# An encoder layer on one core: the sample's pointwise convolution as block-sum products, with the prompt's jobs in another order

## The chip, the cores and the metric

One Trainium2 chip, one core. The metric is device time in microseconds (us) of one launch, the median of the runs shown. The whole layer is one program, and each engine (TensorE or PE, VectorE or DVE, ScalarE or ACT, GpSimd or POOL, SyncE or SP) has a list of instructions of its own.

## The reference

Two sequences, a sample of 1024 tokens and a prompt of 512, go through the same layer with model width 2048:

```python
h = rms_norm(x, norm_g)
z = h @ w_in                                   # 2048 x 5632
c_val, c_glu, c_gate, q, k, v, a_gate = split(z)
# conformer group, 1024 channels
u = c_val * sigmoid(c_glu)
u = depthwise_conv(u, 31 taps) + b_dw
conv_out = (silu(layer_norm(u, ln_g, ln_b)) @ w_pw) * silu(c_gate)    # w_pw 1024 x 1024
# attention group, 8 heads of 128, 2 kv heads, window of 128 keys to each side, a sink per head
attn_out = banded_sink_attention(rope(q), rope(k), v, sink) * silu(a_gate)
y = rms_norm(x + concat(conv_out, attn_out) @ w_out, final_norm_g)    # w_out 2048 x 2048
```

The products are wanted at fp32 accuracy.

## The kernel before, in words

**Three passes for one product.** An fp32 operand is split into a high and a low part: `Encoder.parts` (L446-453) has ACT write the high part with a copy (L449) and DVE the low part with a subtraction (L450). A product is then hi by hi, hi by lo and lo by hi, three matmuls of 128x512 into one PSUM bank. A chunk of weights is loaded into a `raw` tile, and its two parts go into an `hl` tile of 128x1024 each (three such tiles, `NHL`). Tokens sit split in 28 `t` tiles.

**Seven products of block sums.** For the sample's in-projection and out-projection, class `Unit` (L91-250) takes two blocks of output columns, two halves of the inner dimension and two halves of the tokens, and uses the seven products P1 to P7 of sums of blocks in place of eight. The weight side is made in `make0` to `make3`: `make1` subtracts 128x512 blocks (L138), splits the first half of the new operand and then the second. The token sums S1 to S4 and plain blocks A11, A12, A22 are stored, loaded and split (`block_sums`, `load_sum`, `token_sum`). Each product has 12 matmuls (L191), and `tap` and `add` gather the results (L217, L237). Where the order is `ALONE`, it is P1, P2, P6, P5, P7, P3, P4.

**Plain jobs.** A `Job` (L320ff, matmuls at L587) is one block of 128 output columns with 512 tokens: 48 matmuls for the prompt's in-projection, 24 for the pointwise convolution, whose inner dimension is 1024. The sample's pointwise convolution (class `Post`, `first_jobs`) is 16 jobs of 24 matmuls, in two halves of 512 tokens: `prepare` does the layer norm, `normed` stores the result in `cs_d`, `fetch` loads it again and splits it, `pointwise` (L1395) multiplies the product with the gate, and `mixed` stores it.

**Work beside the matmuls.** The depthwise convolution, the attention, the norms and the block sums are generators in three lanes (`attn`, `conv`, `prep`, class `Lane`). After each group of three matmuls `tick` gives every lane credit at its rate, and a lane with credit emits its next step. `drain` or `until` emits all that is left of a lane, or enough of it, at once. One channel block of the depthwise convolution is 31 taps: two on ACT (L912, L913) and 29 on DVE (L917), 128x512 each for the prompt, and a sum (L919). A block of attention is scores (`s`, L1044), mask and maximum on DVE (L1047), exponentials on ACT (L1058), transposes (`pt`, L1078), a split of the transposed block (`a<-pt`) and the products with the values (`pv`, L1073).

**What sets the order.** The code is emitted in one pass, and a scheduler puts each engine's instructions in a fixed list by dependencies and priority. Making weights (`w_prep`, L546) has a priority that moves it up by 400 places of the emitted order (`URGENT`); the high part of a weight chunk is made as soon as an `hl` tile is free. `store_later` and `turn_over` put small steps behind marks. DMAs are issued by SP, each waiting for one that is eight earlier.

**The stages around the change.** The prompt's in-projection (`prompt.jobs`, L1118ff) begins with 12 attention jobs (keys, values, queries) and goes on for eight rounds of GLU, value, conv gate and attention gate. Job 18 (`PM`) calls `prepare`: the sample's convolution is finished, the two layer norms and the first `fetch` go to the prep lane, the sample's gating of the attention (`attention_sums`, L1178) and the prompt's attention groups to the attn lane; the conv lane's rate is 0.5 from there. The prompt's taps enter the conv lane as their value jobs finish. Then come the 16 pointwise jobs, and the eight units of the out-projection on the attention half (`over[0]`) and eight on the convolution half (`over[1]`).

Of the kernel before, what the change touches and what calls it, by code (L numbers as in the profile page):

```python
# [13 lines left out]
P = 128  # L14
# [3 lines left out]
NC = C // P  # L18
# [72 lines left out]
class Unit:  # L91
# [148 lines left out]
    def finish(self, n):  # L240
        e = self.e
        part, d = self.part[n[0]][n[1]], self.d.pop(n)
        if self.total:

            e.add_into(d, part)
            e.later.append([self.landing, self.done(n[0], n[1], d)])
        else:
            e.store_later(part, d)
# [415 lines left out]
class Sequence:  # L664
# [196 lines left out]
    def val(self, i, accs):  # L861
        e, nc = self.e, self.e.nc
        nc.vector.tensor_tensor(self.sig, accs[0], self.sig, ALU.mult)
        e.store_later(self.h_d[i], self.sig, lambda: e.conv.add(self.taps(i)))
# [254 lines left out]
    def jobs(self):  # L1119
# [5 lines left out]
            job(GATE + i, lambda acc: self.silu_out(self.gate_d[i], acc)),  # L1125
# [6 lines left out]
        gate = lambda h: [job(AG + h, lambda acc: self.silu_out(self.ag_d[h], acc))]  # L1132
        attn = kv(0) + kv(1) + sum((query(h) for h in range(HEADS)), [])
        attn[0].before.append(self.rope_tables)
        convs, gates = [conv(i) for i in range(NC)], [gate(h) for h in range(HEADS)]
        return attn + sum((c + g for c, g in zip(convs, gates)), [])


class Mix:
# [55 lines left out]

    def fill(self):

        e = self.e
        e.T = {}
        held = deque()  # L1200

        def load(step):
            if step < 7:
                held.append(self.load_sum(SUMS[ALONE[step]], 1, True, e.F))

        def put(step):
            for j, x in enumerate(held.popleft()):
                self.token_sum(SUMS[ALONE[step]], 1, j, x)

        load(0)  # L1210
        load(1)
        for step in range(4):
            yield 2 * LOAD
            put(step)
            load(step + 2)
        self.put, self.load = put, load
# [82 lines left out]

class Post:  # L1300
# [4 lines left out]
    def __init__(self, e, seq, t0, out):  # L1305
        self.e, self.seq, self.t0, self.out = e, seq, t0, out
        self.cs, self.mix, self.made = {}, {}, {}
        self.cs_d = [e.tc.dram_tile([P, 2, self.N], F32, name=f"cs{seq.s}_{t0}_{i}") for i in range(NC // 2)]
# [52 lines left out]
    def normed(self, i, t):  # L1361
        self.e.store(self.cs_d[i], t)
        self.kept = i + 1

    kept = 0

    def fetch(self):

        e = self.e
        held = deque()  # L1370

        def load(i):
            if i < NC // 2:
                held.append(e.F([2, self.N]))
                e.nc.sync.dma_start(held[-1], self.cs_d[i])

        load(0)
        load(1)
        for i in range(NC // 2):
            yield LOAD  # L1380
            t = held.popleft()
            load(i + 2)
            for j in (0, 1):
                self.cs[2 * i + j] = self.parts(t[:, j])
                yield 1500
# [11 lines left out]

    def mixed(self, i, f):
        self.e.store(self.out.xT[i][:, self.t0 : self.t0 + self.N], f)
# [206 lines left out]
def encoder(ctx, tc, a):  # L1606
# [3 lines left out]
    halves = [Post(e, sample, 0, mix), Post(e, sample, TP, mix)]  # L1610
# [83 lines left out]
    def change(before, unit, nxt):  # L1694

        held = {}
        rooms = (e.F, e.F, e.F, None, e.F, e.F, None)

        def load(step):
            held[step] = mix.load_sum(SUMS[ALONE[step]], 0, False, rooms[step])  # L1700

        def follow(step):
            for j, x in enumerate(held.pop(step)):
                mix.token_sum(SUMS[ALONE[step]], 0, j, x)
            if step < 3:
                load(step + 4)

        def begin():
            e.attn.drain()
            load(2)  # L1710
            load(3)

        before.before.append(e.prep.drain)
        before.after[3] = [lambda: load(0)]
        before.after[5] = [lambda: load(1)]
# [80 lines left out]
    def prepare():  # L1796
# [3 lines left out]
        e.prep.add(halves[0].fetch())  # L1800
# [5 lines left out]
    pace(pj[PM], RATES[4])  # L1806
    jobs = sum(items, []) + [[j] for j in pj]
# [3 lines left out]
    for n, half in enumerate(halves):  # L1811
        fj = half.first_jobs()
# [101 lines left out]
```

## Time and profile before

| | |
|---|---|
| median of 3 runs | 2115.74 us (2115.11 to 2118.36) |
| profiled execution | 2115.94 us, span 2114.2 us, mean granted clock 0.997 |
| PE busy | 2080.8 us, 9330 matmuls |
| DVE busy | 1683.7 us, 2581 instructions |
| ACT busy | 1098.4 us, 1794 instructions |
| last prompt job ends, pointwise begins | 1450.2 us |
| pointwise ends, out-projection begins | 1549.7 us |

The profile is of one execution. Rows of groups give line, engine, operation, tile names and shapes, a count, busy time and mean duration, and then the idle time before them with what ended it. Rows of the timeline give start and duration in us, with the idle time before in brackets. A run of back-to-back instructions is one row with a count, and the start of the next row tells what the run really took, since the durations of successive instructions overlap by some tens of ns. Rows of windows give the busy time of PE, PE's weight loads, DVE, ACT and POOL, then the granted clock, the DMA engines' share and GB/s.

### The profile page before, as it was taken

How to read it: one execution, taken by the hardware profiler on the slowest of the kernel's cores; microseconds unless marked ns; L12 is line 12 of the kernel's file. 1: busy time of each engine (PE TensorE's matmuls, PEld its weight loads, DVE VectorE, ACT ScalarE, POOL GpSimd, SP SyncE). 2: the span in 40 equal slices, each digit the busy share in tenths (PEclk: the TensorE clock that was granted, in tenths of full speed). 3: DMA queues.
4: the chain of work that ended last, by engine and by line, in shares of the span. 5: the costliest groups of instructions: out<-in, count | busy, mean ns of one | idle time of the engine just before them, and what ended most of it. 6: DMA issues, size and time to landing. Idle time of an engine off the chain costs nothing.

```text
span 2114.2 us, 26783 instructions
## 1 busy us (share of the span) xinstructions
PE 2080.8 (98%) x9330; PEld 1708.0 (81%) x9330; DVE 1683.7 (80%) x2581; ACT 1098.4 (52%) x1794; POOL 104.8 (5%) x124
## 2 busy tenths in 40 slices
PE   8999999999999999899999999999999999999998
PEld 7878888888888888688888888777888888887886
DVE  8658799988899898889887775667899677986553
ACT  7475445333555655655556775335454565563232
POOL 0001110000011111000000000000000001110000
PEclk9999999999999999999999999999999999999999
DMA  8888878754667777854465546886877469798962
GB/s 289 305 295 242 229 181 278 263 191 155 216 184 182 185 163 212 268 171 156 151 215 162 192 159 208 315 313 205 265 257 240 135 206 267 189 279 290 314 196 80
DMA packets 236408, 465.17 MB, mean 220 GB/s; under 512 B 22128, under 2 KB 79856, under 8 KB 236272
## 3 DMA queue, kind: packets, MB, share of 16 engines
q1 hardware_dynamic: 218992, 431.99, 61.4%
q0 software_dynamic: 17280, 31.46, 9.3%
q8 instruction: 73, 1.20, 0.2%
q14 instruction: 63, 0.52, 0.1%
HBM read 319.19 MB, written 144.18 MB: 219 GB/s over the span
## 4 chain that ended last, share of the span: by engine, by line
PE 76%; DMA 8%; DVE 7%; issue 5%; ACT 2%; POOL 1%; SPq 1%; ACTq 0%; POOLq 0%; DVEq 0%
PE a L191 22%; PE c L191 11%; PE a L587 10%; PE b L191 6%; PE c L587 5%; PE b L587 5%; DMA a<-ag_d 3%; PE s L1044 2%; PE pv L1073 2%; PE a L1564 2%; PE s L1564 2%; PE s L191 2%; DVE hl L450 2%; DVE f L917 1%; PE pt L1078 1%
## 5 line engine op out<-in xcount | busy, mean ns | idle before, releaser
L191 PE MATMUL a<-t,hl 128*128 128x512 f32 x2640 | 633.3, 390 | 4.6 <-ACT u L217 3.2
L191 PEld LDWEIGHTS a<-t,hl 128*128 128x128 f32 x2640 | 493.8, 188 | 110.8 <-ACT u L217 5.7
L450 DVE TENSOR_TENSOR hl<-raw,hl 128x1024 fp32r<-128x1024 f32 (+1 forms) x330 | 337.7, 1023 | 178.8 <-ACT hl L449 177.9
L449 ACT ACTIVATE hl<-raw 128x1024 fp32r<-128x1024 f32 (+1 forms) x330 | 296.3, 898 | 332.0 <-DVE raw L138 58.0
L917 DVE SCALAR_TENSOR_TENSOR f<-f,c_w_dw,f 128x1024 f32<-128x1024 f32 (+1 forms) x464 | 454.5, 1010 | 1.1 <-ACT f L912 0.8
L587 PE MATMUL a<-t,hl 128*128 128x512 f32 x1344 | 329.2, 394 | 1.2 <-DVE hl L450 0.9
L191 PE MATMUL c<-t,hl 128*128 128x512 f32 x1320 | 318.7, 389 | 0.7 <-ACT g L217 0.7
L587 PEld LDWEIGHTS a<-t,hl 128*128 128x128 f32 x1344 | 248.4, 188 | 53.0 <-DVE hl L450 2.3
L191 PEld LDWEIGHTS c<-t,hl 128*128 128x128 f32 x1320 | 247.7, 188 | 52.8 <-ACT g L217 1.3
L587 PE MATMUL c<-t,hl 128*128 128x512 f32 x672 | 167.3, 396 | 0.7 <-DVE hl L450 0.5
L587 PE MATMUL b<-t,hl 128*128 128x512 f32 x672 | 164.4, 393 | 1.3 <-DVE hl L450 1.3
L191 PE MATMUL b<-t,hl 128*128 128x512 f32 x660 | 161.3, 390 | 0.0
L587 PEld LDWEIGHTS b<-t,hl 128*128 128x128 f32 x672 | 124.4, 188 | 27.0 <-DVE hl L450 2.1
L587 PEld LDWEIGHTS c<-t,hl 128*128 128x128 f32 x672 | 124.7, 189 | 25.8 <-DVE hl L450 1.0
L191 PEld LDWEIGHTS b<-t,hl 128*128 128x128 f32 x660 | 123.4, 188 | 25.2
L217 ACT ACTIVATE u<-a 128x512 f32<-128x512 f32 x114 | 67.4, 592 | 78.8 <-PE a L191 64.4
L217 ACT ACTIVATE g<-a 128x512 f32<-128x512 f32 x106 | 62.8, 592 | 74.9 <-PE a L191 68.2
L1564 PE MATMUL a<-hl,t 128*128 128x512 f32 x192 | 75.0, 390 | 1.6 <-DVE g L1395 1.6
L1058 ACT ACTIVATE p<-p,tiny 128x384 f32<-128x384 f32 (+1 forms) x96 | 54.5, 570 | 33.0 <-DVE tiny L1055 21.8
L346 ACT ACTIVATE hl<-raw 128x1024 fp32r<-128x1024 f32 x44 | 46.3, 1052 | 35.8 <-DMA raw<-w_in 12.8
L449 ACT ACTIVATE a<-pt 128x512 fp32r<-128x512 f32 x64 | 37.9, 592 | 50.4 <-PE pt L1078 50.1
L1047 DVE CUSTOM_DVE_ANT_0 p<-s,c_mask,c_attn_sink 128x384 f32<-128x384 f32 (+1 forms) x96 | 51.0, 568 | 14.9 <-PE s L1044 14.7
(319 smaller groups left out, 2534.9 us busy)
## 6 DMA issues: line engine op xcount, KB each, us to landing
raw<-w_in SPq DMA_DIRECT2D x171, 512.0 KB, 4.8
raw<-w_out SPq DMA_DIRECT2D x64, 256.0 KB, 4.1
raw<-w_out SPq DMA_DIRECT2D x31, 512.0 KB, 5.5
a<-xT_s SPq DMA_DIRECT2D x50, 256.0 KB, 4.7
raw<-w_pw SPq DMA_DIRECT2D x24, 512.0 KB, 4.9
f<-x_s SPq DMA_DIRECT2D x16, 512.0 KB, 6.9
f<-y_d SPq DMA_DIRECT2D x16, 512.0 KB, 5.8
y_s<-f SPq DMA_DIRECT2D x16, 512.0 KB, 4.7
```

The source lines that it names most:

```text
L191: nc.tensor.matmul(acc, hl[:, l, o, j, :], toks[j][:, r], start=name in FRESH and j == 0 and q == 0, stop=name in LAST and j == HALF - 1 a ...
L217: nc.scalar.activation(t, bank, AF.Copy)
L346: e.nc.scalar.activation(t[:, 0], raw, AF.Copy)
L449: nc.scalar.activation(hi, x, AF.Copy)
L450: nc.vector.tensor_tensor(lo, x, hi.bitcast(F32), ALU.subtract)
L587: nc.tensor.matmul(job.acc[0], hl[:, l, kk // HALF, kk % HALF, :], r, start=i == 0 and p == 0, stop=i == nk - 1 and p == 2,)
L917: nc.vector.scalar_tensor_tensor(t, h[:, j : j + T], w(j), t, ALU.mult, ALU.add)
L1044: nc.tensor.matmul(ps[:, 0:n], qs[:, x, h], k[y][:, keys], start=p == 0, stop=p == 2)
L1047: nc.vector.tensor_tensor_reduce(p[:, 0:n], ps[:, 0:n], mask, SCALE, e.sink[:, g * GROUP + h : g * GROUP + h + 1], ALU.add, ALU.max, accum ...
L1058: nc.scalar.activation(p[:, 0:n], p[:, 0:n], AF.Exp, bias=nm[:, h : h + 1], accum_out=l[:, h : h + 1])
L1073: nc.tensor.matmul(pv, v[x][:, vs], pt[:, y], start=i == 0 and p == 0, stop=i == last and p == 2)
L1564: nc.tensor.matmul(acc, self.mix[self.KS[i]][:, m, b * P : (b + 1) * P], part[l].rearrange("p a b -> p (a b)"), start=i == 0 and p == 0, s ...
```

## The change: block sums for the pointwise convolution, and rests for two lanes

- The 16 jobs of the pointwise convolution become four units of seven products, 12 matmuls each: 336 matmuls in place of 384. A new class `Norm` stores the normed tokens (`pair_d`), makes and stores their sums S1 to S4 on the prep lane (`sums`), loads and splits the first three token operands (`fill`), and multiplies the results with the gate (`gated`). The operands of the steps 3 to 6 are put during the last prompt job.
- The prompt's jobs: the 12 attention jobs stay first; then all eight pairs of GLU and value, then all eight pairs of conv gate and attention gate.
- Ahead of the first unit, `rest` emits at once what the attn lane has left until the sample's attention is gated and two blocks of the prompt's attention are finished, and what the conv lane has left until seven of the prompt's eight channel blocks are convolved. During the four units both lanes have rate 0. The eighth channel block's taps enter at `over[0][2]`.
- The conv lane's rate is 1.0 from the twelfth job from the end; `conv_sums` moves to `over[0][1]`; `change`, which refills the token tiles from one unit to the next, now also serves the way from the last pointwise unit to `over[0][0]`.

```diff
         return [
             job(GLU + i, self.glu),
             job(VAL + i, lambda acc: self.val(i, acc)),
-            job(GATE + i, lambda acc: self.silu_out(self.gate_d[i], acc)),
         ]
...
-        convs, gates = [conv(i) for i in range(NC)], [gate(h) for h in range(HEADS)]
-        return attn + sum((c + g for c, g in zip(convs, gates)), [])
+        return attn + sum((conv(i) for i in range(NC)), []) + sum((gate(h) for h in range(HEADS)), [])
...
+class Norm:
+    def sums(self):
+        e, nc = self.e, self.e.nc
+        for j in range(HALF):
+            x = [e.F([TS]) for _ in range(2)]
+            for t, k in zip(x, (j, j + HALF)):
+                nc.sync.dma_start(t, self.xT[k])
+            yield 2 * LOAD
+            self.block_sums(0, j, *x)
+            yield 4000
...
+    def units(self):
+        e = self.e
+        def one(o):
+            done = lambda t, c, z: self.gated(o + c, t, z)
+            return Unit(e, e.a["w_pw"], (o, o + 1), 0, None, done)
+        return [one(o) for o in range(0, NC, 2)]
+
+    def gated(self, o, t, z):
...
+        nc.sync.dma_start(g, self.seq.gate_d[o][:, cols])
+        def steps():
+            nc.vector.tensor_tensor(z, z, g, ALU.mult)
+            yield
+            e.store(self.mix.xT[o][:, cols], z)
...
-        e.prep.add(halves[0].fetch())
+        e.prep.add(norm.sums())
+        e.prep.add(norm.fill())
...
+    pace(pj[-12], RATES[3])
+    def ahead():
+        e.prep.drain()
+        norm.load(3)
+        norm.load(4)
...
+    pj[-2].before.append(ahead)
+    for step in range(3, 7):
+        pj[-1].ticks[HALF * (step - 2) - 1] = lambda step=step: refill(step)
...
+    pw = norm.units()
+    def rest():
+        until(lambda: mix.gated == HALF and prompt.finished >= 2, e.attn)
+        until(lambda: prompt.convolved >= NC - 1, e.conv)
+
+    pw[0].before.append(rest)
+    pace(pw[0], 0.0)
+    pace(pw[0], 0.0, e.attn)
+    jobs += [[u] for u in pw]
...
+    over[0][2].before.append(lambda: e.conv.add(prompt.taps(NC - 1)))
+    over[0][1].before.append(lambda: e.prep.add(mix.conv_sums()))
+    change(pw[-1], pw[-1], over[0][0], 1, (e.F, e.F, None, e.F, e.F, None, e.F))
```

The line numbers of the changed kernel are a few higher than before: L449 and L450 are L450 and L451 there, L917 is L921, L1044 is L1048, L1047 is L1051, L1078 is L1082, L1159 to L1162 are L1164 to L1167, L1178 is L1183.

Three places of the program, as the scheduler leaves them.

First, DVE among the prompt's gate jobs. Before, around the end of the prompt's jobs, its list goes from taps (`f` with `c_w_dw`) and small steps of a softmax to the low parts of two weight chunks (`hl_12230`, `hl_12282`):

```order
L917 SCALAR_TENSOR_TENSOR f_11774<-f_11694,c_w_dw,f_11774 128x512 x6
L1062 TENSOR_TENSOR tiny_11864<-tiny_11864,tiny_11863 128x4
L917 SCALAR_TENSOR_TENSOR f_11774<-f_11694,c_w_dw,f_11774 128x512
L1063 RECIPROCAL tiny_11865<-tiny_11864 128x4
L917 SCALAR_TENSOR_TENSOR f_11774<-f_11694,c_w_dw,f_11774 128x512 x5
L450 TENSOR_TENSOR hl_12230<-raw_12134,hl_12230 128x1024
L450 TENSOR_TENSOR a_12075<-pt_12070,a_12075 128x512
L450 TENSOR_TENSOR hl_12282<-raw_12183,hl_12282 128x1024
```

Now, between the low parts `hl_11896` and `hl_11997`, the first chunks of two successive prompt jobs, DVE has 19 taps, two gate products of the sample's attention (L1183) and twelve instructions of block sums (L1164 to L1167). The end of that stretch:

```order
L921 SCALAR_TENSOR_TENSOR f_11539<-f_11505,c_w_dw,f_11539 128x512 x7
L1164 TENSOR_TENSOR u_11684<-f_11590,f_11591 128x512
L921 SCALAR_TENSOR_TENSOR f_11539<-f_11505,c_w_dw,f_11539 128x512
L1165 TENSOR_TENSOR g_11685<-u_11684,f_11590 128x512
L1167 TENSOR_TENSOR g_11687<-f_11590 128x512
L1166 TENSOR_TENSOR u_11686<-f_11591,g_11685 128x512
L921 SCALAR_TENSOR_TENSOR f_11539<-f_11505,c_w_dw,f_11539 128x512 x2
L451 TENSOR_TENSOR hl_11997<-raw_11899,hl_11997 128x1024
```

What moved: the block sums of the normed tokens and of the attention, with the gate products ahead of them, now stand between two successive weight chunks, where before there were taps and softmax steps.

Second, DVE at the beginning of the pointwise convolution. Before, in its first jobs, each job's weights (`hl_`) follow the last ones after a few other instructions:

```order
L450 TENSOR_TENSOR hl_12376<-raw_12285,hl_12376 128x1024
L1395 TENSOR_TENSOR g_12329<-a_12331,g_12329 128x512
L450 TENSOR_TENSOR hl_12430<-raw_12338,hl_12430 128x1024
L917 SCALAR_TENSOR_TENSOR f_12305<-f_12220,c_w_dw,f_12305 128x512 x2
L450 TENSOR_TENSOR t_1740_12316<-f_12287,t_1740_12316 128x512
L450 TENSOR_TENSOR a_12404<-pt_12399,a_12404 128x512
L450 TENSOR_TENSOR t_1745_12346<-f_12287,t_1745_12346 128x512
L917 SCALAR_TENSOR_TENSOR f_12305<-f_12220,c_w_dw,f_12305 128x512
L1395 TENSOR_TENSOR g_12370<-c_12372,g_12370 128x512
L450 TENSOR_TENSOR hl_12492<-raw_12379,hl_12492 128x1024
```

Now, in the first unit, the operand `hl_12565` is made in two halves (`make1`); its first half and `hl_12573` stand soon after `hl_12442`, and its second half stands at the end of this piece, behind the last taps, token operands (`t_`) and the last three transposed blocks of attention (`a<-pt`):

```order
L451 TENSOR_TENSOR t_1782_12478<-f_12388,t_1782_12478 128x512
L451 TENSOR_TENSOR a_12524<-pt_12519,a_12524 128x512
L451 TENSOR_TENSOR t_1783_12500<-f_12432,t_1783_12500 128x512
L451 TENSOR_TENSOR t_1784_12503<-f_12432,t_1784_12503 128x512
L451 TENSOR_TENSOR t_1785_12506<-f_12433,t_1785_12506 128x512
L451 TENSOR_TENSOR t_1786_12509<-f_12433,t_1786_12509 128x512
L451 TENSOR_TENSOR a_12535<-pt_12530,a_12535 128x512
L138 TENSOR_TENSOR p_12561<-raw_12360,raw_12307 128x512
L138 TENSOR_TENSOR raw_12307<-raw_12307,p_12561 128x512
L451 TENSOR_TENSOR a_12546<-pt_12541,a_12546 128x512
L451 TENSOR_TENSOR hl_12565<-p_12561,hl_12565 128x512
L451 TENSOR_TENSOR hl_12609<-raw_12307,hl_12609 128x512
```

From `hl_12442` (not counted) to the second half of `hl_12565` DVE now has, counted in its list: 58 taps; 37 other instructions of 128x512 (4 subtractions of weight blocks, 20 token operands, 11 low parts of weights, keys, queries and transposed blocks, 2 sums of a channel block); one low part of 128x1024 (`hl_12573`); 8 instructions of mask and maximum; and some 20 of a few elements. The taps of two channel blocks that lay spread between the weights of many jobs now stand in one stretch of the first unit.

Third, PE at the same place. Before, the first pointwise jobs (L587, reading `hl_12230` and the following) have a product of scores between them:

```order
L587 MATMUL b_12278<-t_1585_11242,hl_12230 128x512 x3
L587 MATMUL b_12278<-t_1587_11256,hl_12230 128x512 x3
L587 MATMUL b_12278<-t_1602_11326,hl_12230 128x512 x3
L1044 MATMUL s_12236<-f_11735,a_12153 128x384 x3
L1044 MATMUL s_12242<-f_11735,a_12153 128x384 x3
L587 MATMUL b_12278<-t_1604_11342,hl_12230 128x512 x3
```

Now P1 (`a_12555` from `hl_12442`), P2 and P5 (the first half of `hl_12565`) have been issued with the attention of the two prompt blocks among them, and then P6 needs the second half of `hl_12565`:

```order
L1082 MATMUL pt_12541<-c_ident,p_12401 128x128
L1082 MATMUL pt_12541<-c_ident,p_12407 128x128
L1082 MATMUL pt_12541<-c_ident,p_12450 128x128
L1082 MATMUL pt_12541<-c_ident,p_12456 128x128
L1077 MATMUL pv_12518<-a_12546,f_11840 128x512 x3
L191 MATMUL a_12555<-t_1706_12004,hl_12565 128x512 x3
L191 MATMUL a_12555<-t_1707_12007,hl_12565 128x512 x3
L191 MATMUL a_12555<-t_1708_12010,hl_12565 128x512 x3
L191 MATMUL a_12555<-t_1709_12013,hl_12565 128x512 x3
```

On PE, 36 matmuls of the first unit and the attention of two prompt blocks stand between the last prompt job and P6: 12 score products of 256 and 12 of 384, 20 transposes and 15 products with the values.

More of the change, by code (lines that the diff above doesn't have):

```diff
@@ L241, in finish @@
         e = self.e
-        part, d = self.part[n[0]][n[1]], self.d.pop(n)
+        d = self.d.pop(n)
+        part = self.part and self.part[n[0]][n[1]]
         if self.total:
-            e.add_into(d, part)
+            if part is not None:
+                e.add_into(d, part)
             e.later.append([self.landing, self.done(n[0], n[1], d)])
@@ L863, in val @@
         nc.vector.tensor_tensor(self.sig, accs[0], self.sig, ALU.mult)
-        e.store_later(self.h_d[i], self.sig, lambda: e.conv.add(self.taps(i)))
+        if i < NC - 1:
+            e.store_later(self.h_d[i], self.sig, lambda: e.conv.add(self.taps(i)))
+        else:
+            e.store_later(self.h_d[i], self.sig)
     def gated(self, i):
@@ L1361, in normed @@
     def normed(self, i, t):
[L1362 to L1385, printed above, removed]
+        self.e.store(self.out.pair_d[i][:, :, self.t0 : self.t0 + self.N], t)
     def parts(self, f):
@@ L1692, in switch, with change @@
             u.after.setdefault(at, []).append(lambda step=step: follow(step))
-    def change(before, unit, nxt):
+    def change(before, unit, nxt, g, rooms):
         held = {}
-        rooms = (e.F, e.F, e.F, None, e.F, e.F, None)
+        ahead = 4 if before is not unit else 3
         def load(step):
-            held[step] = mix.load_sum(SUMS[ALONE[step]], 0, False, rooms[step])
+            held[step] = mix.load_sum(SUMS[ALONE[step]], g, False, rooms[step])
         def follow(step):
             for j, x in enumerate(held.pop(step)):
-                mix.token_sum(SUMS[ALONE[step]], 0, j, x)
-            if step < 3:
-                load(step + 4)
+                mix.token_sum(SUMS[ALONE[step]], g, j, x)
+            if step + ahead < 7:
+                load(step + ahead)
         def begin():
-            e.attn.drain()
-            load(2)
-            load(3)
+            if before is not unit:
+                e.attn.drain()
+            else:
+                load(0)
+                load(1)
+            for step in range(2, ahead):
+                load(step)
         before.before.append(e.prep.drain)
-        before.after[3] = [lambda: load(0)]
-        before.after[5] = [lambda: load(1)]
+        if before is not unit:
+            before.after.setdefault(3, []).append(lambda: load(0))
+            before.after.setdefault(5, []).append(lambda: load(1))
         unit.before.append(begin)
```

85 lines of the change are left out of this document (43 added, 42 removed).

## The prediction

> **What bounds the kernel now.** I read the profile's page first: the busy times, the slices of the span and the chain that ended last.
>
> ```profile
> PE 2080.8 (98%) x9330; PEld 1708.0 (81%) x9330; DVE 1683.7 (80%) x2581; ACT 1098.4 (52%) x1794; POOL 104.8 (5%) x124
> PE   8999999999999999899999999999999999999998
> DVE  8658799988899898889887775667899677986553
> PE 76%; DMA 8%; DVE 7%; issue 5%; ACT 2%; POOL 1%; SPq 1%; ACTq 0%; POOLq 0%; DVEq 0%
> ```
>
> TensorE is busy for 98% of the span, so a matmul saved is worth its time only if PE finds the next one ready. VectorE has 20% of room over the whole, but its slices go from 5 to 9 tenths, so I asked for the stretch that the change touches: the last prompt jobs (to 1450 us) and the pointwise convolution (1450 to 1550). The columns are length, busy PE, PEld, DVE, ACT and POOL, clock, DMA share and GB/s.
>
> ```profile
> 1340.00:1360.00 20.00, 20.00 (x89) 16.55 (x89) 16.45 (x26) 4.65 (x6) 0.00 (x0) 1.00 0.99 343
> 1360.00:1380.00 20.00, 19.27 (x84) 15.31 (x83) 5.35 (x6) 6.08 (x8) 0.00 (x0) 1.00 0.82 292
> 1480.00:1500.00 20.00, 19.98 (x91) 16.59 (x90) 19.35 (x36) 6.00 (x13) 0.00 (x0) 1.00 0.80 254
> 1560.00:1580.00 20.00, 19.82 (x89) 15.75 (x88) 19.93 (x32) 7.91 (x12) 0.00 (x0) 1.00 0.84 279
> ```
>
> In the pointwise stage and behind it DVE is full (19.35 and 19.93 of 20 us) and PE loses next to nothing. That works only because, in DVE's list, the weights' low parts never have more in front of them than PE can cover. What PE waits for in the last prompt jobs (1300 to 1445) is small:
>
> ```profile
> PE s L1044 <- ACT a L449: 2.6, 1, 2.6
> PE b L587 <- DVE hl L450: 0.6, 1, 0.6
> PE c L587 <- DVE hl L450: 0.5, 1, 0.5
> PE a L587 <- DVE hl L450: 0.5, 1, 0.5
> PE a L587 <- ACT hl L449: 0.2, 1, 0.2
> ```
>
> Does DVE run its list in the order in which it stands? The timeline of DVE around 1443 has a low part of weights, a transposed block and the next low part, as the piece of the list from before has them:
>
> ```profile
> 1413.47 4.73 DVE L917 SCALAR_TENSOR_TENSOR f<-f,c_w_dw,f 128x512 f32<-128x512 f32 x7
> 1418.11 1.22 DVE L450 TENSOR_TENSOR hl<-raw,hl 128x1024 fp32r<-128x1024 f32 x1
> ...
> 1443.79 1.21 DVE L450 TENSOR_TENSOR hl<-raw,hl 128x1024 fp32r<-128x1024 f32 x1
> 1444.93 0.68 DVE L450 TENSOR_TENSOR a<-pt,a 128x512 fp32r<-128x512 f32 x1
> 1445.53 1.21 DVE L450 TENSOR_TENSOR hl<-raw,hl 128x1024 fp32r<-128x1024 f32 x1
> ```
>
> It does, and these rows give the real cost of an instruction from start to start: 4.64 us for 7 taps, 0.66 each; 1.14 for a 128x1024 low part (1443.79 to 1444.93); 0.60 for a 128x512 one (1444.93 to 1445.53). [...]
>
> **The change, part by part.** *Matmuls removed.* The timeline of PE gives the pace:
>
> ```profile
> 1306.37 11.04 PE L587 MATMUL b<-t,hl 128*128 128x512 f32 x48
> 1317.25 11.04 PE L587 MATMUL a<-t,hl 128*128 128x512 f32 x48
> ```
>
> 48 matmuls take 10.88 us from start to start, 0.2267 each. Of 384 go 48: -10.9 us. The list of PE is otherwise of the same length. The evacuations, the gate products and the splitting of the normed tokens that are exchanged for others are work of DVE and ACT beside the matmuls: at 0.60 and 1.14 us I count about 37 us of DVE work gone (16 low parts of 1024, the 16 halves of the fetched tokens, 16 gate products) and some 71 added (four units at about 11, sums of the normed tokens, 28 token operands). It costs nothing where PE has cover, and I look for the places where it hasn't.
>
> *The drain ahead of the first unit.* This is the main term. The low part of P1's operand (`hl_12442`) can't be made before the last job but one has ended, since ACT copies that job's result first in its list. From there: 0.6 for that copy, 1.06 and 1.14 for the two parts, 2.8 us. Behind it, up to the second half of `hl_12565`, stands the stretch counted above. For a bound from above I take the mean durations of groups (1250 to 1900 us), which count the overlap twice:
>
> ```profile
> L917 DVE SCALAR_TENSOR_TENSOR f<-f,c_w_dw,f 128x512 f32<-128x512 f32 x167 | 117.4, 743 | 0.2
> L450 DVE TENSOR_TENSOR t<-f,t 128x512 fp32r<-128x512 f32 x72 | 46.7, 683 | 5.1 <-ACT t L449 5.1
> L1047 DVE CUSTOM_DVE_ANT_0 p<-s,c_mask,c_attn_sink 128x384 f32<-128x384 f32 x20 | 11.5, 611 | 3.6 <-PE s L1044 3.6
> L1047 DVE CUSTOM_DVE_ANT_0 p<-s,c_mask,c_attn_sink 128x256 f32<-128x256 f32 x20 | 8.8, 479 | 7.1 <-PE s L1044 7.1
> L217 ACT ACTIVATE g<-a 128x512 f32<-128x512 f32 x106 | 62.8, 592 | 74.9 <-PE a L191 68.2
> ...
> 1322.89 1.06 ACT L449 ACTIVATE hl<-raw 128x1024 fp32r<-128x1024 f32 x1 [2.47 <-PE a L587]
> ```
>
> 58 taps at 0.66 are 38.5; 37 instructions of 128x512 at 0.60 are 22.2; one of 1024, 1.1; the mask and maximum, 4 at 0.48 and 4 at 0.61, 4.4; the tiny ones about 1: 67 us, and with 2.8 ahead 70 us after the last job but one. (At mean durations 75 and 78.) In that time PE can do: the last prompt job, 10.9; P1, P2 and P5, 36 matmuls, 8.2; and the attention of two blocks. For that the groups of PE are:
>
> ```profile
> L1073 PE MATMUL pv<-a,f 128*128 128x512 f32 x60 | 19.4, 401 | 0.1
> L1078 PE MATMUL pt<-c_ident,p 128*128 128x128 f32 x100 | 16.8, 274 | 0.1
> L1044 PE MATMUL s<-f,a 128*128 128x384 f32 x48 | 10.0, 340 | 0.0
> L1044 PE MATMUL s<-f,a 128*128 128x256 f32 x48 | 8.1, 300 | 2.6 <-ACT a L449 2.6
> ```
>
> 15, 20, 12 and 12 of these are 4.9 + 3.4 + 2.5 + 2.0 = 12.8 us busy, with overlap in it; 15 products at 0.2267 are 3.4, and scaled alike the others make it 9. So PE has 28 us of work in 70: it stands still for 42 us ahead of P6. Upper bound: 78 less 28, and up to 5 for links of the softmax that DVE itself waits for (ACT's exponentials, a transpose, a split), 55. Lower: if `hl_12442` were made half a job sooner (5.4) and the attention took the whole 12.8, 33. I take 42 and 3 for the links. The cover was the 16 plain jobs, which in the old order took the taps in small pieces between weights. What this work leaves free later brings nothing: in the out-projection PE didn't wait for DVE.
>
> *The pile among the gate jobs.* A job's first chunk is split when an `hl` tile gets free, in the middle of the job before (the row at 1322.89: 5.6 us into the job that began at 1317.25). From the making of `hl_11896` (1.06 and 1.14) through 19 taps (12.5), 12 instructions of 128x512 (7.2), two gate products (2.3) and `hl_11997` (1.1) DVE needs 25.3 us; PE has half a job and a job, 16.3. So 9 us of waiting. Ends: 3.6 if `hl_11896` is made half a job sooner, or nothing if DVE gets it earlier still; above, the gate products' loads can be late. In the old order they were:
>
> ```profile
> DVE a L1178 <- DMA a<-ag_d: 25.3, 7, 6.0
> ```
>
> Two such waits of 6.0 bring it to 21. I take 9.
>
> *The old waits.* 4.4 us in the five rows above, and a dip of the clock:
>
> ```profile
> 1429.77 0.74 PE L1044 MATMUL s<-f,a 128*128 128x256 f32 x4 [2.60 <-ACT a L449]
> ...
> 1428.00:1431.00 3.00, 1.23 (x6) 1.10 (x7) 1.38 (x2) 2.52 (x3) 0.00 (x0) 0.92 1.08 378
> 1431.00:1434.00 3.00, 3.00 (x12) 2.55 (x10) 0.90 (x4) 0.02 (x1) 0.00 (x0) 0.51 0.15 55
> ```
>
> After a wait of 2.60 us the clock is at 0.51 for one stretch of 3 us: about 1.5 us lost. With the jobs in another order these 5.9 us may go or return elsewhere; I take half, -3, between 0 and -6.
>
> *The clock.* By the same rows each long wait costs 1.5 us when dense work resumes: twice, +3 (0 to 5). [...]
>
> *The sum*, against the profiled execution of 2115.94 us (the median of the runs is 0.2 us lower): 2115.9 - 10.9 + 42 + 3 + 9 - 3 + 3 = 2159 us. The ends: 2115.9 - 10.9 + 33 + 0 + 0 - 6 + 0 = 2132, and 2115.9 - 10.9 + 55 + 21 - 0 + 5 = 2186.
>
> **The rivals.** *Covered after all (faster).* DVE's full windows at 1480 and 1560 show that a backlog need not reach PE. If the taps of the drain stand where DVE would have idled anyway, and the low parts are early, then 48 matmuls and the old waits go: 2115.9 - 10.9 - 5.9 = 2099, or 2108 with the pile among the gate jobs. For it speaks 5.35 of 20 us busy at 1360, so there is room just ahead; against it, that room lies in front of `hl_12442`, and the list puts the taps behind. It decides if the drain holds less than 11 us more than PE's 28.
>
> *The transfers bind (slower still).* The stretch of the prompt's jobs gets 4 MB of loads and 4 MB of stores for the sums of the normed tokens and 7 MB of token operands, and loses 4 MB of `fetch`: 11 MB net. At 320 GB/s, between the 292 and 343 above, that is 34 us of transfers, and in 140 us with a share of 0.82 to 0.99 there is room for about 14. The other 20 would come on top: 2179.
>
> *A short drain.* If the first pile stays hidden and the drain costs its lower bound, 2115.9 - 10.9 + 33 - 3 = 2135.
>
> *Nothing to be seen.* The drain costs as much as is saved, 11 to 17 us: 2116.
>
> **How the numbers follow.** The forecast has 0.67: its working rests on counts in a list and durations that hold for hundreds of instructions. Covered after all, 0.13; the transfers, 0.10; the short drain, 0.07; nothing to be seen, 0.03. A difference of 0.2%, 4.2 us, is about what a measurement of this kernel can tell from none. So faster 0.13, same 0.03, slower 0.84. The range goes from 2126, a little below the low end of the forecast, to 2188, above its high end; it leaves out the covered case and the one with nothing to be seen, 0.16.
>
> **What would show it.** In the profile of the changed kernel: 9282 matmuls; a stretch of 60 to 80 us in which DVE is full and PE is busy for less than half, right behind the last prompt job, with P6 (L191, `a<-t,hl`) released by DVE's `hl` after tens of us in which PE had only attention; a wait of 5 to 15 us of an L588 matmul for DVE's `hl` some 40 us ahead of it; a lower clock behind each; and a lighter DVE in the out-projection with no gain there. The prediction is wrong if PE's waits for DVE stay under 15 us in all, or if P6 is released early; and its first term is wrong if the four units take more than 76 us (336 at 0.2267) without waits of PE.

## The result, and the profile after

The changed kernel takes 2175.19 us (median of 5 runs, 2173.53 to 2179.95), against 2116.98 us before (5 runs, 2115.11 to 2118.36): a ratio of 1.028, interval 1.027 to 1.029. It is slower by 58 us, where the prediction had 43, in a range of 2126 to 2188.

The page of the changed kernel, with the rows that answer to those shown of before: the busy times, and the slices of PE, DVE and the granted clock.

```profile
span 2171.7 us, 26845 instructions
...
PE 2088.0 (96%) x9282; PEld 1709.1 (79%) x9282; DVE 1717.6 (79%) x2641; ACT 1104.7 (51%) x1822; POOL 104.9 (5%) x124
...
PE   8999999999999999999999999784999999999998
DVE  8657898988998888988987786669588877887553
...
PEclk9999999999999999999999999895899999999999
```

The 48 matmuls are gone (9282 of 9330). Apart from the first and the last slice, PE is below 9 tenths only in slices 26 to 28, the stretch from 1357 to 1520 us; the clock is low in slices 26, 28 and 29. The rest of the program is full as it was.

What PE waits for, over the whole span: engine, line, releaser, then us in total, times and the longest. None of these three is among the waits of before.

```profile
PE pt L1082 <- ACT p L1069: 20.1, 2, 14.5
PE a L588 <- ACT g L930: 19.9, 3, 13.5
PE c L191 <- DVE t L451: 8.0, 1, 8.0
```

The windows of 20 us (busy PE, PEld, DVE, ACT, POOL, then clock, DMA share and GB/s) show two separate holes.

```profile
1360.00:1380.00 20.00, 18.37 (x81) 14.87 (x80) 9.52 (x18) 5.21 (x6) 0.00 (x0) 1.00 0.89 295
1380.00:1400.00 20.00, 6.53 (x24) 5.04 (x24) 11.79 (x16) 3.08 (x4) 0.00 (x0) 0.69 1.03 407
...
1460.00:1480.00 20.00, 10.33 (x50) 7.94 (x48) 20.00 (x39) 4.19 (x6) 0.00 (x0) 0.82 0.18 62
1480.00:1500.00 20.00, 8.73 (x21) 5.36 (x21) 18.96 (x33) 10.34 (x25) 0.00 (x0) 0.50 0.34 105
1500.00:1520.00 20.00, 8.70 (x22) 5.95 (x22) 17.94 (x37) 9.44 (x22) 0.00 (x0) 0.59 0.42 125
```

They look different. From 1460 to 1520 DVE is full, ACT and the DMA engines are not, and PE is busy for half or less: DVE is what is late. From 1380 to 1400 DVE and ACT are idle for long and the DMA engines are busy throughout (share 1.03, 407 GB/s; the same window of before had 0.88 and 292): there late transfers are the first suspect.

The timeline of PE through both, with the idle time before a row and its releaser in brackets:

```profile
1362.19 11.22 PE L588 MATMUL a<-t,hl 128*128 128x512 f32 x48 [1.63 <-ACT g L930]
1373.25 11.04 PE L588 MATMUL c<-t,hl 128*128 128x512 f32 x48
1397.76 12.74 PE L588 MATMUL a<-t,hl 128*128 128x512 f32 x48 [13.47 <-ACT g L930]
1410.33 0.61 PE L588 MATMUL b<-t,hl 128*128 128x512 f32 x2
1413.14 10.72 PE L588 MATMUL b<-t,hl 128*128 128x512 f32 x46 [2.19 <-DVE hl L451]
1428.62 12.65 PE L588 MATMUL a<-t,hl 128*128 128x512 f32 x48 [4.75 <-ACT g L930]
1441.11 11.04 PE L588 MATMUL c<-t,hl 128*128 128x512 f32 x48
1451.99 8.78 PE L588 MATMUL a<-t,hl 128*128 128x512 f32 x38
...
1463.93 2.88 PE L191 MATMUL a<-t,hl 128*128 128x512 f32 x12
...
1485.18 1.68 PE L1082 MATMUL pt<-c_ident,p 128*128 128x128 f32 x4 [14.53 <-ACT p L1069]
...
1529.65 5.13 PE L191 MATMUL a<-t,hl 128*128 128x512 f32 x12 [1.17 <-ACT u L217]
1534.62 1.09 PE L191 MATMUL c<-t,hl 128*128 128x512 f32 x4
```

Among the gate jobs PE stands for 1.63 + 13.47 + 2.19 + 4.75 = 22.0 us, and two jobs behind long waits take 12.6 and 12.5 us from start to start in place of 10.88 (3.3 us; the clock was 0.50 from 1398 to 1401 and 0.57 from 1428 to 1431). The last prompt job starts at 1451.99, P1 at 1463.93 and P6 at 1529.65. Between P1 and P6 lie 65.7 us, for 36 matmuls (8.2 us) and the attention of two blocks (about 9). P6's own 12 matmuls take 4.97 us in place of 2.72. PE's own long waits in it are booked to ACT (14.53 us ahead of the transposes), but ACT stood behind DVE: its exponential waited for a step of the softmax that has taps in front of it and behind it in DVE's list. ACT's row and DVE's:

```profile
1479.71 0.51 ACT L1062 ACTIVATE p<-p,tiny 128x256 f32<-128x256 f32 x1 [7.37 <-DVE tiny L1059]
...
1479.66 4.05 DVE L921 SCALAR_TENSOR_TENSOR f<-f,c_w_dw,f 128x512 f32<-128x512 f32 x6
...
1484.36 0.17 DVE L1067 RECIPROCAL tiny<-tiny 128x4 f32<-128x4 f32 x1
```

The last part of DVE's timeline ahead of P6:

```profile
1495.61 8.69 DVE L921 SCALAR_TENSOR_TENSOR f<-f,c_w_dw,f 128x512 f32<-128x512 f32 x13
1504.22 2.48 DVE L451 TENSOR_TENSOR t<-f,t 128x512 fp32r<-128x512 f32 x4
...
1511.64 2.49 DVE L451 TENSOR_TENSOR t<-f,t 128x512 fp32r<-128x512 f32 x4
...
1519.48 0.69 DVE L451 TENSOR_TENSOR a<-pt,a 128x512 fp32r<-128x512 f32 x1
...
1525.19 0.69 DVE L138 TENSOR_TENSOR p<-raw,raw 128x512 f32<-128x512 f32 x1 [1.53 <-PE pt L1082]
1525.91 0.69 DVE L138 TENSOR_TENSOR raw<-raw,p 128x512 f32<-128x512 f32 x1
1526.52 0.68 DVE L451 TENSOR_TENSOR a<-pt,a 128x512 fp32r<-128x512 f32 x1
1527.12 0.68 DVE L451 TENSOR_TENSOR hl<-p,hl 128x512 fp32r<-128x512 f32 x1
```

These are 13 taps back to back, token operands, transposed blocks, and last the second half of the operand (`hl<-p`), at 1527.12: the order of the list.

### The profile page after: what moved, and what is told of

It is laid out like the page before. It is cut to its first block, busy times and chain, and to the rows that moved or that the text cites. A ratio compares the mean times of both kernels' runs of the same rounds, so it can differ in the third digit from the quotient of the medians.

```text
span 2171.7 us, 26845 instructions
## 1 busy us (share of the span) xinstructions
PE 2088.0 (96%) x9282; PEld 1709.1 (79%) x9282; DVE 1717.6 (79%) x2641; ACT 1104.7 (51%) x1822; POOL 104.9 (5%) x124
## 4 chain that ended last, share of the span: by engine, by line
PE 77%; DMA 8%; DVE 7%; issue 5%; ACT 2%; SPq 1%; POOL 1%; ACTq 0%; POOLq 0%; DVEq 0%
PE a L191 25%; PE c L191 12%; PE a L588 10%; PE b L191 6%; PE c L588 5%; PE b L588 4%; PE s L191 3%; PE pv L1077 2%; DVE f L921 2%; PE s L1048 2%; DMA raw<-w_out 2%; DMA f<-y_d 1%; PE pt L1082 1%; DMA a<-ag_d 1%; DVE hl L451 1%
## 5 line engine op out<-in xcount | busy, mean ns | idle before, releaser
L451 DVE TENSOR_TENSOR hl<-raw,hl 128x1024 fp32r<-128x1024 f32 (+1 forms) x330 | 333.0, 1009 | 201.6 <-ACT hl L450 200.6
L450 ACT ACTIVATE hl<-raw 128x1024 fp32r<-128x1024 f32 (+1 forms) x330 | 292.9, 888 | 332.7 <-DVE raw L138 62.8
L921 DVE SCALAR_TENSOR_TENSOR f<-f,c_w_dw,f 128x1024 f32<-128x1024 f32 (+1 forms) x464 | 452.6, 1009 | 1.5 <-ACT f L916 1.4
L588 PE MATMUL a<-t,hl 128*128 128x512 f32 x1152 | 286.5, 399 | 21.8 <-ACT g L930 19.9
L191 PE MATMUL b<-t,hl 128*128 128x512 f32 x708 | 173.2, 390 | 0.0
L191 PEld LDWEIGHTS b<-t,hl 128*128 128x128 f32 x708 | 132.5, 188 | 27.2
L588 PE MATMUL b<-t,hl 128*128 128x512 f32 x576 | 141.5, 394 | 2.8 <-DVE hl L451 2.8
L588 PEld LDWEIGHTS b<-t,hl 128*128 128x128 f32 x576 | 106.5, 188 | 25.0 <-DVE hl L451 3.7
L217 ACT ACTIVATE g<-a 128x512 f32<-128x512 f32 x114 | 67.5, 592 | 86.8 <-PE a L191 80.5
L217 ACT ACTIVATE u<-a 128x512 f32<-128x512 f32 x122 | 72.0, 591 | 76.1 <-PE a L191 70.6
L1082 PE MATMUL pt<-c_ident,p 128*128 128x128 f32 x256 | 50.3, 286 | 20.2 <-ACT p L1069 20.1
L450 ACT ACTIVATE a<-pt 128x512 fp32r<-128x512 f32 x64 | 38.0, 594 | 53.2 <-PE pt L1082 52.9
```

Source lines behind the costliest of these rows:

```text
L191: nc.tensor.matmul(acc, hl[:, l, o, j, :], toks[j][:, r], start=name in FRESH and j == 0 and q == 0, stop=name in LAST and j == HALF - 1 a ...
L217: nc.scalar.activation(t, bank, AF.Copy)
L450: nc.scalar.activation(hi, x, AF.Copy)
L451: nc.vector.tensor_tensor(lo, x, hi.bitcast(F32), ALU.subtract)
L588: nc.tensor.matmul(job.acc[0], hl[:, l, kk // HALF, kk % HALF, :], r, start=i == 0 and p == 0, stop=i == nk - 1 and p == 2,)
L921: nc.vector.scalar_tensor_tensor(t, h[:, j : j + T], w(j), t, ALU.mult, ALU.add)
```

## The experiments

In all of them the theory is that PE waits for a weight's low part, or for an evacuation, behind what the lists of DVE and ACT hold in front of it. The rivals are named in each. Intervals are 95% on the ratio to the kernel before, measured beside it.

**The order of the jobs alone (e1).** The kernel before, with the prompt's job list of the changed one:

```diff
             job(VAL + i, lambda acc: self.val(i, acc)),
-            job(GATE + i, lambda acc: self.silu_out(self.gate_d[i], acc)),
...
+            job(GATE + h, lambda acc: self.silu_out(self.gate_d[h], acc)),
             job(AG + h, lambda acc: self.silu_out(self.ag_d[h], acc)),
```

> The kernel before, with the prompt's jobs in the changed order and nothing else changed. Theory A (the loss comes from what DVE's list holds between two chunks of weights): in this kernel's list no chunk has more than 10.3 us of DVE work in front of it around the end of the prompt's jobs, so 2113 to 2121 us, the same as before. Rival B (the 22 us of waits among the gate jobs come from the order of the jobs by itself, since all results that ACT evacuates through the four g tiles and stores now come one behind another): about 2117 + 22 = 2139 us.

Measured 2112.48 us against 2116.57; ratio 0.998 (0.9975 to 0.9994). The new order costs nothing by itself; the median is about 4 us lower. Of PE's waits between 1300 and 1445, five rows and 4.4 us before, one is left:

```profile
PE s L1044 <- ACT a L449: 2.2, 1, 2.2
```

So the order alone doesn't make those 22 us of waits, and it takes half of the old ones away. This kernel is the only one in this document whose median lies below that of before.

**Attention behind the units (e2).** The prompt's attention is added at `over[0][0]`, and the rest waits for the sample's gating alone:

```diff
-        for group in prompt.groups:
-            e.attn.add(group)
...
-        until(lambda: mix.gated == HALF and prompt.finished >= 2, e.attn)
-        until(lambda: prompt.convolved >= NC - 1, e.conv)
+        until(lambda: mix.gated == HALF, e.attn)
...
+    over[0][0].before.append(lambda: [e.attn.add(group) for group in prompt.groups])
```

> The changed kernel with the prompt's attention added behind the pointwise units and the wait for two finished blocks of it left out of the rest; the taps stay as they are. The list has 37 us of DVE work (42 taps) in one stretch in front of a chunk of the first unit, where the changed kernel has 13 and 50 (56 taps and attention), and 18 in front of a gate job's chunk in place of 23. Theory A: the wait ahead of P6 becomes some 20 us shorter and the one among the gate jobs about 5: 2145 to 2155 us. Rival C (the waits are the links of the softmax, not the taps: without attention nothing holds P6): about 2175 - 50 = 2125 us.

Measured 2173.92 us (ratio 1.028, 1.026 to 1.029). Both expectations fail. The longest wait in the first unit is now this one, and a wait of 4.15 us stands ahead of it. PE waits for a token operand, which stands in DVE's list behind 37 taps with one sum among them:

```profile
1502.23 5.06 PE L191 MATMUL c<-t,hl 128*128 128x512 f32 x11 [19.73 <-DVE t L451]
```

```profile
1476.37 8.70 DVE L921 SCALAR_TENSOR_TENSOR f<-f,c_w_dw,f 128x512 f32<-128x512 f32 x13
...
1485.58 15.99 DVE L921 SCALAR_TENSOR_TENSOR f<-f,c_w_dw,f 128x512 f32<-128x512 f32 x24
1501.48 2.50 DVE L451 TENSOR_TENSOR t<-f,t 128x512 fp32r<-128x512 f32 x4
```

Rival C is out: there is no softmax left in front of it, and PE still waits for DVE. But the time didn't fall: PE no longer had the attention's matmuls to do in the hole and has them to do later, and where they are done there is a new hole:

```profile
1760.00:1780.00 20.00, 13.39 (x46) 8.45 (x44) 7.62 (x20) 8.99 (x22) 0.00 (x0) 0.67 0.32 105
```

One of the two lines that e2 alters in `rest` did nothing in the changed kernel. The line that emits taps until seven channel blocks are done emits none: without that line alone the program is the same, instruction for instruction. When the code gets there the conv lane is empty; the rate of 1.0 from the twelfth job from the end had emitted the taps already. Of the attention, `rest` emits five steps.

**The rate kept at 0.5 (e3).** Without the line that raises it, the rest has two channel blocks of taps to emit:

```diff
-    pace(pj[-12], RATES[3])
```

> The changed kernel without the line that sets the convolution's rate to 1.0 from the twelfth prompt job from the end: it stays 0.5, and the rest now has taps to emit at once. Theory A': it isn't the emission at once that counts but how much DVE has in its list; by the list 12.9 and 35.5 us stand in front of the two halves of the operand (13.2 and 49.9 in the changed kernel), and 16.6 in front of a gate job's chunk (23.4): about 14 and 7 us less, 2150 to 2158 us. Rival D (the emission at once by the rest is what costs, as the prediction put it): with more to drain the time rises above 2175 us.

Measured 2187.7 us (1.035, 1.033 to 1.036), on the side of rival D. But the trace says why in another way. P1 starts at 1462.43 and P6 at 1511.07, 48.6 us apart in place of 65.7: the hole shrank by 17 us, as the list had it (14). The loss came back elsewhere: 6.72 us behind DVE's token operands at 1588, and at the prompt's layer norm, which waits until the last taps are done:

```profile
PE s L632 <- ACT u L450: 13.5, 1, 13.5
```

**Spread thin (e4).** The rate 0.3 from the twelfth job from the end, 0.4 in the units, no drain, attention behind as in e2:

```diff
-    pace(pj[-12], RATES[3])
+    pace(pj[-12], 0.3)
...
-    pace(pw[0], 0.0)
+    pace(pw[0], 0.4)
```

> The changed kernel with the convolution at rate 0.3 from the twelfth prompt job from the end and 0.4 during the units, nothing drained, and the prompt's attention behind the units. In its list no chunk has more than 12.6 us of DVE work in front of it. Theory A: the long waits go and the 48 matmuls are saved: 2106 to 2116 us. Rival E (transfers of the block sums, or ACT's evacuations, hold the gate jobs): 15 to 25 us more, 2125 to 2140 us.

Measured 2168.15 us (1.025, 1.023 to 1.027), worse than either expected. The first unit is nearly free of waits, 3.2 us in all up to 1481. But the gate jobs keep theirs (1.63, 13.04 and 4.77), so the taps' rate isn't their cause. And the attention that was moved behind has a drain of its own before `over[0][7]`, where PE is idle for more than 5 of 10 us:

```profile
1750.00:1760.00 10.00, 4.74 (x20) 2.88 (x19) 3.66 (x14) 5.59 (x16) 0.00 (x0) 0.87 0.28 79
```

**Two pieces of work left out (e5, e7, e8).** e5 leaves out the block sums of the normed tokens, e7 the prompt's taps on DVE, e8 both; what these kernels return isn't the layer's result.

```diff
# e5: Norm.sums
-            for t, k in zip(x, (j, j + HALF)):
-                nc.sync.dma_start(t, self.xT[k])
-            yield 2 * LOAD
-            self.block_sums(0, j, *x)
+        for n in ("S1", "S2", "S3", "S4"):
+            self.sums_d[0, n] = [self.xT[j][:, :W] for j in range(HALF)]
# e7: Sequence.taps
+            if T == TS:
                 nc.vector.scalar_tensor_tensor(t, h[:, j : j + T], w(j), t, ALU.mult, ALU.add)
```

> The changed kernel with the block sums of the normed tokens left out (their 4 MB of loads, 16 DVE instructions and 4 MB of stores; the units read plain blocks in their place, in loads of the same size). Theory F (the waits among the gate jobs come from the new sums: DVE stands behind late loads of the normed tokens, and ACT's evacuations behind that): the 22 us of waits there and some 3 us of lower clock go, and the list has 25 us less in front of the first unit's operand (8.5 and 28.9 in place of 13.2 and 49.9), so 2120 to 2132 us. Rival G (they come from 16 gate jobs in a row, each with a result to store): the waits for ACT's g tiles stay at about 20 us and the time is over 2140 us.

Measured 2144.79 us (1.014, 1.012 to 1.016), over rival G's bound of 2140; but the waits among the gate jobs don't stay at 20 us, as G has it: they fall to 1.71, 1.58 and 7.88. P1 to P6 falls to 39.7 us from 65.7, 26 less, as the list had it (25).

> The changed kernel with the 29 DVE taps of each of the prompt's channel blocks left out (ACT's two taps and the sums of a block remain; the lanes are paced as if the taps were there). Theory A (the taps in front of the second half of P6's operand are the wait): what is left in front of it is 18 us and some 10 more, about what PE has to do, so the 50 us ahead of P6 shrink to under 10, and the waits among the gate jobs to some 15: 2110 to 2130 us. Rival C (links of the softmax and loads that come late, with the taps running in time that DVE would have waited anyway): over 2150 us.

Measured 2146.0 us (1.014, 1.012 to 1.016), between the two. P1 to P6 is 36.6 us, 29 less than in the changed kernel, where the taps left out are 38.5 us of DVE's work: with them gone, a link of the softmax shows, a wait of 6.92 us ahead of the transposes. The waits among the gate jobs stay at 0.63, 14.81 and 4.51: no tap is needed for them.

> Both left out, the block sums of the normed tokens and the prompt's taps on DVE. If these two are all that costs, the 48 matmuls show: 2117 - 11 = 2106 us, less the old waits 2100. Rival J (the four units cost something themselves, by their evacuations, sums and gate products): over 2112 us.

Measured 2119.37 us (1.001, 1.000 to 1.003). Without both, the kernel is level with before. P1 to P6 is 23.7 us, 6.5 more than PE's own work. The profile of e8 has no wait over 3 us in the two places. The time is over rival J's bound of 2112 all the same: 13 us are missing to 2106. In the trace 6.5 us of it are that hole, which is links of the softmax, and 2.3 the clock behind it; two waits of 1.63 us for evacuations in the gate jobs and one of 2.92 us for attention are some more. By the pages, PE is idle for 6.5 us more than before, and of the 10.9 us of saved matmuls 4.1 go to a lower clock (a mean of 0.995 in place of 0.997), which leaves 0.3 saved. Whether the units bring these waits with them stays open.

Against the changed kernel, e5 takes away 30.4 us, e7 29.2 and e8 55.8: the two pieces of work together account for nearly all of the loss, about half each. e5 leaves out the sums' transfers and their work on DVE at once, so no run parts these two.

**What holds the gate jobs (e6, e9, e11).** e6 keeps the new sums out of the `g` tiles that the evacuations use; e9 gives a channel block's load four times the lead; e11 puts the prompt's jobs back in the old order.

```diff
# e6: Norm.block_sums
-        s1, s2, s4, s3 = (e.E() for _ in range(4))
+        s1, s2, s4, s3 = (e.U([W], F32) for _ in range(4))
# e9: Sequence.taps
-        yield LOAD
+        yield LOAD if T == TS else 4 * LOAD
```

> The changed kernel with the results of the normed tokens' block sums in u tiles alone, not in g and u by turns; g tiles then serve the evacuations of the gate jobs and every second sum of the attention. The same transfers and the same DVE work. Theory H (what holds ACT's evacuations is that the sums occupy g tiles): the 20 us of waits for ACT's g go, 2148 to 2156 us. Theory I (what holds them is the order of the lists, DVE behind late loads and ACT behind DVE, wherever the sums are kept): 2170 to 2180 us, as the changed kernel.

Measured 2175.36 us (1.028, 1.026 to 1.030): which tiles the sums are kept in doesn't matter. The longest wait among the gate jobs is 14.01.

> The changed kernel with one number changed: after the load of a prompt channel block the convolution waits for 18 us of lane time in place of 4.5 before its first taps on ACT and DVE. Theory K (the longest wait among the gate jobs is ACT's evacuation standing behind the first taps of a channel block, whose load comes late among the loads of the block sums): that wait of 13.5 us goes or falls under 5, with the clock's dip behind it. The list also changes in front of the first unit's operand, to 18.8 and 32.2 us from 13.2 and 49.9, some 12 us less of waiting: 2145 to 2158 us in all. Rival L (the gate jobs are held by the transfers as such, whichever instruction is behind them): the waits for ACT's g stay near 20 us and only the 12 us go, 2160 to 2166 us.

Measured 2203.1 us (1.040, 1.038 to 1.041), worse than both. Theory K falls: the wait stays, 14.13, and another grows to 9.53. In the changed kernel ACT's evacuation stood behind the first taps (L916), the first two rows; here, in the third, ACT waits for a `g` tile itself, until a sum's store has gone:

```profile
1394.37 0.81 ACT L916 ACTIVATE f<-f,c_b_dw,c_w_dw 128x512 f32<-128x512 f32 x1 [8.99 <-DVE a L1183]
...
1397.11 0.60 ACT L930 ACTIVATE g<-a 128x512 f32<-128x512 f32 x1 [1.31 <-DVE f L921]
...
1398.57 0.60 ACT L930 ACTIVATE g<-a 128x512 f32<-128x512 f32 x1 [12.30 <-DMA nsum_S<-g]
```

With one of these holds removed, the next one is as late. What they have in common stands above them in DVE's timeline, here that of the changed kernel: between two low parts of weights it stands still for loads of the normed tokens and of the gates, 8.1 us, and the sums and their stores come behind. In e6, e9 and e11 it stands still there for the same loads for 9.9, 10.2 and 9.2 us.

```profile
1379.98 1.23 DVE L451 TENSOR_TENSOR hl<-raw,hl 128x1024 fp32r<-128x1024 f32 x1 [4.70 <-ACT hl L450]
1385.48 0.69 DVE L1164 TENSOR_TENSOR u<-f,f 128x512 f32<-128x512 f32 x1 [4.27 <-DMA f<-norm_d]
...
1393.07 1.23 DVE L1183 TENSOR_TENSOR a<-a,a 128x1024 f32<-128x1024 f32 x1 [3.84 <-DMA a<-ag_d]
...
1411.87 1.22 DVE L451 TENSOR_TENSOR hl<-raw,hl 128x1024 fp32r<-128x1024 f32 x1
```

The list was right about the first unit: P1 to P6 is 47.2 us, 18 less (12 by the list). But the later taps brought 13.6 us behind token operands at 1604 and 15.3 us at the layer norm, as in e3.

> The changed kernel with the prompt's jobs in the order of before (GLU, value, conv gate and attention gate by turns). The list has about the same piles, 24.1 us among the last jobs and 12.5 and 50.5 in the first unit. If the piles and the loads cost, whatever the jobs are: 2170 to 2180 us. If the row of 16 gate jobs is a condition of the waits for ACT's g: 15 to 25 us less, 2150 to 2160 us.

Measured 2178.59 us (1.028, 1.027 to 1.030), as the first of the two has it. A wait of 14.52 us for ACT's `g` is there with the old order too.

**Spread further (e10).** e4 with e9's lead, rates 0.5 in the units and 0.7 behind, attention at 2.5.

```diff
-    pace(pw[0], 0.0)
+    pace(pw[0], 0.5)
...
+    pace(over[0][0], 2.5, e.attn)
```

> The changed kernel with the four times longer lead of the taps, the convolution at 0.3 in the gate jobs, 0.5 in the units and 0.7 behind, nothing drained, and the prompt's attention behind the units at rate 2.5. The list has at most 16.7 us in front of a chunk among the gate jobs and 9.8 behind them. If piles in the list and the late load are all that costs: 2106 to 2118 us. If DVE's and ACT's work that was moved behind only makes its waits there (as with the slow convolution, 2168 us): over 2135 us.

Measured 2196.6 us (1.037, 1.036 to 1.039), as the second has it. The first unit has waits of 2.5 us in all, and one wait at the prompt's layer norm is 37.7 us long:

```profile
1877.76 1.52 PE L632 MATMUL s<-u,ones_r 128*128 128x512 f32 x2 [37.66 <-ACT u L450]
```

**The same work sooner (e12).** The norms, the sums, the gating and the prompt's attention go to the lanes at job 13, and with them the conv lane's rate of 0.5 begins five jobs sooner:

```diff
-PM = 18
+PM = 13
```

> The changed kernel with the layer norms, the sums, the sample's gating of the attention and the prompt's attention given to the lanes at the prompt's job 13 in place of 18, 54 us of matmuls sooner; nothing is left out. In the list DVE has 36 us between the first low part of the first unit and the second half of P6's operand, where the changed kernel has 67, and 18 in place of 23 in the pile among the gate jobs. Theory A (piles in DVE's list and the crowd of transfers are all that costs): the wait ahead of P6 shrinks by some 30 us to about 15, the waits among the gate jobs shrink or go: 2125 to 2145 us. Rival J (the units' own evacuations and sums cost as much wherever the rest stands): over 2160 us.

Measured 2145.17 us (1.013, 1.011 to 1.015), the upper end of theory A's range and 30 us less than the changed kernel with nothing left out. Waits of 5.45 and 4.95 us are left among the gate jobs, and P1 to P6 is 37.1 us:

```profile
1390.78 12.92 PE L588 MATMUL a<-t,hl 128*128 128x512 f32 x48 [5.45 <-ACT g L930]
1434.44 1.23 PE L1048 MATMUL s<-f,a 128*128 128x256 f32 x4 [4.95 <-ACT a L450]
1471.82 4.93 PE L191 MATMUL c<-t,hl 128*128 128x512 f32 x11 [4.78 <-DVE t L451]
```

Part of the crowd now stands between 1240 and 1300, where the DMA engines' share is 0.69 to 0.92 and was 0.31 to 0.58 in the changed kernel. So about half of the loss depends on where the same work stands. With the sums and the taps left out (e8) the units are level with the plain jobs; no run made them a gain.

## Why the prediction was right, and where not

- **The matmuls saved, -10.9.** Right: 9282, and a prompt job still takes 10.88 us from start to start.
- **The wait ahead of P6, 42 and 3 for links.** The mechanism held and the size nearly. P6 was forecast 70 to 73 us after the end of the last job but one and came 77.7 after (1451.99 to 1529.65); by the prediction's own 28 us of PE work, 49.6 of waiting in place of 45. From the end of P1's low part (1454.9) to that of P6's second half (1527.7) DVE took 72.8 us: 5.1 of waiting in it, and 67.7 of work where 67 were counted. So the links were 5 and not 3, and P6 came 1.9 us later still, behind ACT's evacuation of P1's bank. Of the 49.6 us PE stood still for 34.7; the other 15 or so are its own work at a lower clock (0.50 to 0.82 in the windows), which DVE's list covered. The signs came only in part: P6 is released by ACT (`u`), not by DVE's `hl`, and by the names in PE's rows its waits for DVE are 16.6 us in all, little over the 15 below which the prediction was to be wrong, since the profile books most of the hole to ACT's softmax step, which stood behind DVE's taps.
- **The origin of that pile** was stated wrongly. The prediction has `rest` emit the taps at once. It emits none, and the pile was in the list already, from the rate of 1.0 in the last 12 jobs. The count of the list was right whoever emitted it, and this is why the time came out. e3, where the drain is real, made the hole shorter, not longer. The prediction also says that what this work leaves free later brings nothing; the other way round, work that was moved later cost time: e3, e9 and e10 show waits of 13.5, 15.3 and 37.7 us at the prompt's layer norm when taps are put behind.
- **The pile among the gate jobs, +9.** The term was too small: 22.0. The pile itself stood as counted: from 1379.98 to the end of the low part at 1411.87 DVE has 24.9 us of work (24.2 counted) and 8.1 of waiting for two loads. What was missed is a second hold beside it: 19.9 of the 22.0 us are PE waiting for a free PSUM bank, the evacuation (L930) being late on ACT, and only 2.19 are booked to the low part. The two run side by side and can't be added. Had the bank been free at 1384.3, where the wait of 13.47 us begins, PE would have done one job of 10.9 and then stood until the low part was there at 1413.1, some 18 us by estimate. The upper bound of 21, from late loads, was the truer value, and the rival of the transfers belonged in the main line: e5 without the sums' loads and stores has 11 us there, e7 without taps still 20, all of it at the bank.
- **The old waits, -3.** They were 5.9 with the clock's dip, and the 22.0 above are now all the waits of that stretch. e1 shows about 4 us given by the new order alone.
- **The clock, +3.** 1.7, 1.6 and 2.25 us behind three waits (13.47, 4.75 and, at P6, 1.17, with the clock at 0.50 from 1529 to 1532): 5.6, beside the 15 or so inside the hole. The wait of 4.75 us cost about as much as that of 13.47; behind the wait of 2.19 us the clock was 1.00 (1413 to 1419). The 0 at the lower end of the term didn't come: behind both waits of over 4 us among the gate jobs the clock was low, 0.50 and 0.57.
- **The sum.** -10.9 + 49.6 + 22.0 + 5.6 - 5.9 = +60.4 against 57.5 us of longer span; the attention's 9 us is an estimate, and the rest is within it. From the pages alone: PE is idle for 83.7 us of the span in place of 33.4, +50.3, and busy for 7.2 more though 10.9 of matmuls are gone, so 18.1 went to a lower clock (a mean of 0.981 in place of 0.997): -10.9 + 50.3 + 18.1 = +57.5. All of the terms that cost were too small, the gate jobs' most of all. The result lies in the range by its width, and nearer to the rival of the transfers (2179) than to the forecast (2159).

The faster rival is out: nothing covered the pile, though DVE was busy for only 10 of 20 us just ahead of it (1440 to 1460); the taps stand in the list behind a low part that waits for ACT, and ACT for PE (4.70 us ahead of the low part at 1453.76).

## What to carry to other kernels

Count what the lists of DVE and ACT hold in front of each weight's last part, in us, against what PE has to do until then. A stretch that was longer (67.7 us of DVE's work ahead of P6, against 28 of PE's) stopped PE here even though DVE had been busy for only 10 of 20 us shortly before. The name beside a wait was the last link only: 14.53 us stood under ACT, which waited for DVE behind its taps. Follow it back. Before saving matmuls that need sums of their inputs, ask where the loads and stores of those sums go: the stage that took them here had a DMA share of 0.82 to 0.99 already. And the taps that were moved out of the full stage had a deadline further on, the prompt's layer norm, with waits of 13.5, 15.3 and 37.7 us there (e3, e9, e10); look for such a deadline before moving.

## What was not expected of the hardware

The DMA engines' share went to 1.03 at 407 GB/s in the window 1380 to 1400, with 8.15 MB moved in place of 5.84. A 512 KB load of the gates took 8.4 us from issue to landing there, at the median; in the same window of before it took 7.5. A 512 KB chunk of weights took 8.4 in place of 6.7, and 19 transfers were issued in the window in place of 17. When the changed kernel was altered around the late evacuation (e6, e9, e11), the longest wait of PE among the gate jobs stayed at 14.0, 14.1 and 14.5 us. In e6 and e11 the evacuation stands behind the first taps (L916) as in the changed kernel, in e9 behind a store of a sum, and in all of them DVE waits for the same loads just before. Which single transfer comes first in that chain wasn't tried and stays open.
